# One decoder trunk, one change: a warmed opening, a written order around the last scan, weight tiles moved by 128 bytes, two output queues

## The chip, the core and the metric

The kernel runs on one core of one Trainium2 chip. The metric is the device time of one execution in microseconds (us). Three runs of the kernel before took 1699.51, 1695.92 and 1690.34 us, a median of 1695.92 us.

## What is computed

A trunk of four layers on 512 positions of width 1024, in float32: dilated attention, a gated FFN, a Mamba-2 scan mixer, a second gated FFN, then a last normalization. Cut to what matters:

```
for i in range(2):
    h = rmsnorm(x, mix_norm_w[i])
    if i == 0: x = x + dilated_attention_mixer(h, w_qkv, w_o, cos, sin)   # 3 groups of windows, 8 heads
    else:      x = x + ssd_mixer(h, w_in, ..., norm_w, w_out)             # 8 groups, 4 chunks of 128
    h = rmsnorm(x, ffn_norm_w[i])
    u = causal_depthwise_conv(h @ w_up, conv_w, conv_b)                   # 1024 -> 2 x 2816
    gate, up = u[..., :2816], u[..., 2816:]
    x = x + (silu(gate) * up) @ w_down
return rmsnorm(x, final_norm_w)
```

In the scan mixer a group's output `y` is gated, divided by the root mean square over its 256 channels, and multiplied by `w_out`.

## The kernel before

**Tiling.** Features stand on the 128 partitions and positions on the free axis, so x is eight tiles `xr[0..7]` of 128x512 and each weight unit is a 128x1024 tile, eight blocks of 128x128. Every large product is made of three matmuls (`mm3`, line 128): a float32 operand is split into a rounded part `h` and a remainder `l`, and the sum h·h + h·l + l·h is accumulated in one PSUM bank. Each of these matmuls has 512 columns and comes from one helper (line 126).

**Weights.** `load_unit` (line 107) loads a unit `raw` by DMA on SP's queue, casts it to `hi` on ACT (on DVE where it is loaded in pieces, which only the opening does) and subtracts to `lo` on DVE. There are four `hi` and four `lo` buffers and three `raw` ones.

**Rows.** `prep(k)` (line 169) turns one tile of x into the rows of the next product: `xh[k]` (ACT), `xl[k]` (DVE), its square (ACT) and the square's addition to `ssum` (POOL, line 182). When all eight are added, `inv_rms` sums over the partitions with matmuls against ones (`ss`, line 190), DVE scales (`ms`), POOL takes the power (`rcol`, line 195), and `along_free` (line 201) spreads the result with matmuls on an identity (`rb`). The product itself runs on rows that are not yet normalized; only its evacuation waits for `rb`.

**Stages.** The opening (lines 263 to 282) loads the eight tiles of x and the first four units of the values' weights, `v_steps`, in which the x tile is the stationary operand and the weights are the moving one (`v`, 96 matmuls a pass, four passes in all: two before the heads, two woven into them). Then come eight heads of attention (`qk`, `wo`), FFN 0 (`u`, `wd`), the scan mixer in eight groups (`xs`, `z`, `wso`, with the scan's own small matmuls `py`, `pf`, `pst`, `ss`, `prg`), and FFN 1. The output product of group 7, `wso70` to `wso77` (`write_groups([7])`), can't start before that group's `y70`, `y71` are normalized, and each `wso7m` must be added to `xr[m]` and prepared before the first product of FFN 1 can read `xh[m]`, `xl[m]`. `norm_and_project` (line 146) then does the first three units of FFN 1, `u1_0` to `u1_2`: seven eighths of the first two, the remaining eighths, `ss`, 15 matmuls of the third, `rb`.

**What sets the order.** A scheduler with a simulated timeline orders each engine's instructions; only inside `tc.manual_schedule` is an engine's order the one that is written. PSUM has three `mm` banks, three `aux` banks and two `side` banks.

**The end.** `finish` (line 805) does the last down products in two halves of 256 positions. For each half: `ss` over two operands in turn (lines 190 and 192), `rc`, `rb`, eight multiplications into four tiles `ot` (five on DVE at line 835, three on POOL at line 833), and four output DMAs, all on SP's queue (line 836).

## Time and profile before

| what | us | share |
|---|---|---|
| the three runs, median | 1695.92 | |
| the profiled execution, its own time | 1691.93 | |
| its span in the trace | 1690.1 | 100% |
| PE (matmuls), 8208 | 1658.2 | 98% |
| DVE, 1791 | 1085.5 | 64% |
| ACT, 1016 | 690.1 | 41% |
| POOL, 312 | 478.8 | 28% |
| DMA engines, mean | | 29% |

The page gives each engine's busy time, the granted TensorE clock in forty slices, the chain of work that ended last, and the costliest groups of instructions. The span is what the trace shows; the time of the execution is 1.8 us longer than it. PE is the engine to look at, so the views that matter are those of its timeline: where it is idle and for what, and how far apart the starts of two successive matmuls are, which is called the pitch here.

### The profile page before, as it was taken

Reading aid. Unit: us, or ns where it says so; the run is one execution under the profiler, and the core shown is the slowest. Engines: PE = TensorE matmul, PEld = TensorE weight load, DVE = VectorE, ACT = ScalarE, POOL = GpSimd, SP = SyncE. Lnnn points to the kernel's source line nnn. Section 1 sums busy time; section 2 is a strip of 40 time slices with the busy share of each in tenths; the row PEclk is TensorE's granted clock in tenths of the full one; section 3 lists DMA queues with packets and bytes.
Section 4 is the critical chain, followed back from the end, with each engine's and each line's share of the span. In section 5 each row is a group of like instructions: output and inputs, shape, how many; then the busy total and the mean of one; then the engine's idle time right before and its main releaser. Section 6 shows DMA issues by size and latency. Waiting matters only on the chain. (4 is left out here: it accounts for less than half of the span.)

```text
span 1690.1 us, 21485 instructions
## 1 busy us (share of the span) xinstructions
PE 1658.2 (98%) x8208; PEld 1399.0 (83%) x8208; DVE 1085.5 (64%) x1791; ACT 690.1 (41%) x1016; POOL 478.8 (28%) x312
## 2 busy tenths in 40 slices
PE   8999999999999999999999999999999999999997
PEld 6888888888888888888888788888887788888887
DVE  6365665366657745745657888788786774574565
ACT  4233332333344423433445665544562442342345
POOL 2344443044413211210231223232312421121124
PEclk9999999999999999999999999999999999999999
DMA  6222222222233223323233322233222222322324
GB/s 211 100 75 88 76 87 87 88 75 88 75 100 113 100 87 112 100 88 112 79 103 127 100 88 100 88 113 102 98 94 75 76 99 87 112 100 88 112 79 134
DMA packets 52343, 165.56 MB, mean 98 GB/s; under 512 B 5841, under 2 KB 8145, under 8 KB 52241
## 3 DMA queue, kind: packets, MB, share of 16 engines
q1 hardware_dynamic: 52240, 164.19, 29.0%
q8 instruction: 65, 1.06, 0.3%
q14 instruction: 38, 0.30, 0.1%
HBM read 162.01 MB, written 2.16 MB: 97 GB/s over the span
## 5 line engine op out<-in xcount | busy, mean ns | idle before, releaser
L126 PE MATMUL u<-xl,hi_u 128*128 128x512 f32 x704 | 271.3, 385 | 4.1 <-DVE xl L171 4.1
L126 PE MATMUL u<-xh,hi_u 128*128 128x512 f32 x704 | 271.1, 385 | 0.0
L126 PE MATMUL u<-xh,lo_u 128*128 128x512 f32 x704 | 270.8, 385 | 0.0
L517 POOL TENSOR_TENSOR au<-au,au 128x512 f32<-128x512 f32 x44 | 57.0, 1294 | 434.3 <-DVE au L497 413.7
L310 POOL TENSOR_TENSOR rotqk<-rotqk,sr 32x512 f32<-32x512 f32 x48 | 91.8, 1913 | 262.8 <-DVE rotqk L309 215.5
L117 ACT CAST hi_u<-raw_u 128x1024 fp32r<-128x1024 f32 x88 | 91.1, 1042 | 183.4 <-PE u L126 122.6
L497 DVE SCALAR_TENSOR_TENSOR au<-usu,par,au 128x511 f32<-128x511 f32 (+1 forms) x176 | 161.4, 921 | 6.4 <-ACT au L495 1.3
L126 PEld LDWEIGHTS u<-xl,hi_u 128*128 128x128 f32 x704 | 132.3, 188 | 30.8 <-DVE xl L171 5.6
L126 PEld LDWEIGHTS u<-xh,lo_u 128*128 128x128 f32 x704 | 132.4, 188 | 25.5
L126 PEld LDWEIGHTS u<-xh,hi_u 128*128 128x128 f32 x704 | 132.3, 188 | 25.4
L126 PE MATMUL qk<-xh,hi_qk 128*128 128x512 f32 x384 | 149.1, 388 | 0.0
L126 PE MATMUL qk<-xl,hi_qk 128*128 128x512 f32 x384 | 148.1, 386 | 0.0
L126 PE MATMUL qk<-xh,lo_qk 128*128 128x512 f32 x384 | 147.1, 383 | 0.0
L512 DVE TENSOR_TENSOR usu<-u,rbc 128x512 f32<-128x512 f32 x88 | 60.7, 691 | 118.0 <-PE u L126 111.5
L118 DVE TENSOR_TENSOR lo_u<-raw_u,hi_u 128x1024 fp32r<-128x1024 f32 x88 | 110.0, 1254 | 26.9 <-ACT hi_u L117 26.9
L530 DVE TENSOR_TENSOR xr<-xr,wd 128x512 f32<-128x512 f32 x40 | 27.2, 687 | 117.1 <-PE wd L126 117.1
L117 ACT CAST hi_qk<-raw_qk 128x1024 fp32r<-128x1024 f32 x48 | 50.2, 1046 | 127.9 <-PE qk L126 73.1
L117 ACT CAST hi_wd<-raw_wd 128x1024 fp32r<-128x1024 f32 (+1 forms) x56 | 52.5, 953 | 119.1 <-PE wd L126 74.8
L306 DVE TENSOR_TENSOR qk<-qk,cr 128x512 f32<-128x512 f32 x48 | 33.0, 688 | 91.0 <-PE qk L126 90.8
L182 POOL TENSOR_TENSOR ssum<-ssum,sq 128x512 f32<-128x512 f32 (+1 forms) x40 | 56.0, 1400 | 106.8 <-ACT sq L181 105.8
L126 PEld LDWEIGHTS qk<-xh,lo_qk 128*128 128x128 f32 x384 | 72.0, 188 | 13.2
L126 PEld LDWEIGHTS qk<-xh,hi_qk 128*128 128x128 f32 x384 | 72.1, 188 | 12.8
(631 smaller groups left out, 4013.0 us busy)
## 6 DMA issues: line engine op xcount, KB each, us to landing
raw_u<-in_wup SPq DMA_DIRECT2D x88, 512.0 KB, 3.2
raw_qk<-in_wqk SPq DMA_DIRECT2D x48, 512.0 KB, 3.2
raw_wd<-in_wdn SPq DMA_DIRECT2D x32, 512.0 KB, 3.2
raw_wd<-in_wdn SPq DMA_DIRECT2D x24, 384.0 KB, 3.0
raw_xs<-in_win SPq DMA_DIRECT2D x16, 512.0 KB, 3.3
raw_z<-in_win SPq DMA_DIRECT2D x16, 512.0 KB, 3.2
lm<-rows SPq DMA_DIRECT2D x32, 256.0 KB, 3.7
raw_wso<-in_wso SPq DMA_DIRECT2D x16, 512.0 KB, 3.2
```

The source lines that it names most:

```text
L117: SC.copy(hi[:, s], raw[:, s])
L118: low.tensor_tensor(lo[:, s], raw[:, s], hi.bitcast(F32)[:, s], op=ALU.subtract)
L126: T.matmul(in_turns(dst), w, in_turns(x), start=first, stop=last)
L182: G.tensor_tensor(ssum, ssum, sq, op=ALU.add)
L306: V.tensor_tensor(at(t), of(p), of(cr), op=ALU.mult)
L310: G.tensor_tensor(rot[R, :], rot[R, :], sr[R, :], op=ALU.mult)
L497: V.scalar_tensor_tensor(dst[:, j:], src[:, : S - j], col(c_w + taps - 1 - j), dst[:, j:], op0=ALU.mult, op1=ALU.add,)
L512: V.tensor_tensor(us, p, rbc, op=ALU.mult)
L517: G.tensor_tensor(ab[1], ab[0], ab[1], op=ALU.mult)
L530: V.tensor_tensor(xr[m], xr[m], p, op=ALU.add)
```

## The change

- **Opening.** Eight matmuls of `ones` on `ones` (`warm`) stand first on PE. `prep` is divided into `split` (`xh`, `xl`) and `square`; the opening writes all the splits first, and the seven additions of squares go to DVE instead of POOL. The second half of each unit's `hi` is cast on ACT instead of DVE (four casts).
- **Weight tiles.** `hi` and `lo` are 1088 elements wide in place of 1024, and the values' units start 32 elements (128 bytes) into them. A smaller DMA scratch makes the room. Every tile's address changes with it.
- **`inv_rms`.** All matmuls over the first operand, then all over the second; one start and one stop for the bank.
- **Last scan.** `last_group` writes PE's order by hand from the second half of group 7's scan on: the group's sum of squares (`ss`) stands behind `wso55`, its `prg` between `wso56` and `wso57`; `u1_0` to `u1_2` are woven into `wso73` to `wso77`, with `u1_1` and `u1_2` in the two `side` banks; the FFN's `ss` comes behind all 72 matmuls of these three. The two casts `y70h`, `y71h` are written ahead of the two subtractions `y70l`, `y71l`.
- **Output.** Of each half's four output DMAs, two are issued on ACT's queue.

Everything else keeps its order, apart from two swaps of neighbours on DVE and one on SP.

```diff
-    def load_unit(src, name, n=1024, pieces=1, low=V):
+    def load_unit(src, name, n=1024, pieces=1, low=V, at=0):
...
-        hi = wh.tile([P, 1024], F32R, tag="hi", name=f"hi_{name}")
-        lo = wh.tile([P, 1024], F32R, tag="lo", name=f"lo_{name}")
+        hi, lo = (wh.tile([P, 1088], F32R, tag=t, name=f"{t}_{name}")[:, at : at + 1024] for t in ("hi", "lo"))
...
-            if pieces > 1:
+            if i < pieces - 1:
                 V.tensor_copy(hi[:, s], raw[:, s])
             else:
                 SC.copy(hi[:, s], raw[:, s])
...
-    def square(k, src, ssum):
+    def square(k, src, ssum, add=G):
...
-            G.tensor_tensor(ssum, ssum, sq, op=ALU.add)
+            add.tensor_tensor(ssum, ssum, sq, op=ALU.add)
...
-        for j in range(cn):
-            js = slice(j * P, (j + 1) * P)
-            T.matmul(p[:, j : j + 1], ssum[:, js], ones[:, 0:1], start=True, stop=more is None)
-            if more is not None:
-                T.matmul(p[:, j : j + 1], more[:, js], ones[:, 0:1], start=False, stop=True)
+        parts = [ssum] if more is None else [ssum, more]
+        for i, part in enumerate(parts):
+            for j in range(cn):
+
+                T.matmul(
+                    p[:, j : j + 1], part[:, j * P : (j + 1) * P], ones[:, 0:1], start=i == 0 and j == 0,
+                    stop=i == len(parts) - 1 and j == cn - 1, skip_group_check=True,
+                )
...
-                state[u] = load_unit(A["wv"][((g - 1) * 2 + half) * 4 + u], f"{n}{u}", pieces=pieces)
+                state[u] = load_unit(A["wv"][((g - 1) * 2 + half) * 4 + u], f"{n}{u}", pieces=pieces, at=32)
...
+    warm = side_bank("warm")
+    for _ in range(8):
+        T.matmul(warm[:, 0:P], ones, ones, start=True, stop=True)
...
-            prep(k, xp, C_MIX, ssum)
+            split(k, xp, C_MIX)
+            xps.append(xp)
...
+    for k, xp in enumerate(xps):
+        square(k, xp, ssum, V)
...
+    def last_group():
...
+        scan = scan_group(NSG - 1, tiles[NSG - 1], ys)
+        weave(scan, 3, ahead[NSG - 1][4:] + w4 + w56[:4])
+        load7, w7 = write_groups([7], ys)
+        with tc.manual_schedule(engines={mybir.EngineType.PE}):
+            next(scan)
+            w56[4]()
+            w56[5]()
+            next(scan)
+            w56[6]()
+            load7(0)
...
+            with tc.manual_schedule(engines={mybir.EngineType.DVE, mybir.EngineType.Activation}):
+                next(scan, None)
+                w56[7]()
+                unit(0)
+                load7(1)
+            w7[0]()
+            w7[1]()
+            w7[2]()
+            part(0, 0)
+            w7[3]()
+            part(0, 1)
+            part(1, 0, 1)
+            w7[4]()
+            part(0, 2)
+            part(1, 2)
+            part(2, 0)
+            w7[5]()
...
+            w7[7]()
+            part(2, 4)
+            for k in range(5, KD):
+                for i in range(3):
+                    part(i, k)
+            inv_rms(ssum_b, D, rcol)
+            part(3, *range(4))
+            p = along_free(rcol, "rb")
+            SC.copy(rbc, p)
+            part(3, *range(4, KD))
...
-                dma(out[k : k + 2, :, ts].rearrange("k p t -> p k t"), ot.rearrange("p (k t) -> p k t", k=2))
+                queue = nc.sync if k % 4 == 0 else nc.scalar
+                queue.dma_start(out[k : k + 2, :, ts].rearrange("k p t -> p k t"), ot.rearrange("p (k t) -> p k t", k=2))
...
-    nc = bacc.Bacc("TRN2", target_bir_lowering=False, num_devices=1)
+    nc = bacc.Bacc("TRN2", target_bir_lowering=False, num_devices=1, dynamic_dma_scratch_size=1024)
```

Three places show how the built programs differ. A row is an instruction: its line, its operation, what it writes and what it reads. The first place is DVE in the opening, from its first work on; `hi_v`, `lo_v` are the values' weights, `xl` the remainders of x. Before:

```order
L115 CAST hi_v_114<-raw_v_113 128x512
L171 SCALAR_TENSOR_TENSOR xl_90<-xp_108,par,xh_82 128x512
L118 TENSOR_TENSOR lo_v_115<-raw_v_113,hi_v_114 128x512
L115 CAST hi_v_114<-raw_v_113 128x512
L118 TENSOR_TENSOR lo_v_115<-raw_v_113,hi_v_114 128x512
L171 SCALAR_TENSOR_TENSOR xl_91<-xp_122,par,xh_83 128x512
L115 CAST hi_v_165<-raw_v_164 128x512
L171 SCALAR_TENSOR_TENSOR xl_92<-xp_157,par,xh_84 128x512
L115 CAST hi_v_165<-raw_v_164 128x512
L118 TENSOR_TENSOR lo_v_166<-raw_v_164,hi_v_165 128x512 x2
L171 SCALAR_TENSOR_TENSOR xl_93<-xp_173,par,xh_85 128x512
```

And after:

```order
L116 CAST hi_v_122<-raw_v_121 128x512
L176 SCALAR_TENSOR_TENSOR xl_90<-xp_117,par,xh_82 128x512
L119 TENSOR_TENSOR lo_v_123<-raw_v_121,hi_v_122 128x512 x2
L176 SCALAR_TENSOR_TENSOR xl_91<-xp_130,par,xh_83 128x512
L186 TENSOR_TENSOR ssum<-ssum,sq 128x512
L116 CAST hi_v_167<-raw_v_166 128x512
L176 SCALAR_TENSOR_TENSOR xl_92<-xp_162,par,xh_84 128x512
L186 TENSOR_TENSOR ssum<-ssum,sq 128x512
L119 TENSOR_TENSOR lo_v_168<-raw_v_166,hi_v_167 128x512 x2
L176 SCALAR_TENSOR_TENSOR xl_93<-xp_175,par,xh_85 128x512
L186 TENSOR_TENSOR ssum<-ssum,sq 128x512
```

One cast of every unit has left DVE's row, and one addition of squares has come in behind each `xl` from the second on.

The second place is DVE at the end of the last scan, where `yt` are the two halves of group 7's output, `wso57` is the last product of groups 5 and 6, and `lo_u1_*`, `lo_wso71` are remainders of weights. Before:

```order
1253 L754 SCALAR_TENSOR_TENSOR yt_10106<-yt_10106,par_76,prg_10307 128x512
1254 L754 SCALAR_TENSOR_TENSOR yt_10188<-yt_10188,par_76,prg_10307 128x512
1255 L118 TENSOR_TENSOR lo_u1_0_10480<-raw_u1_0_10478,hi_u1_0_10479 128x1024
1256 L775 TENSOR_TENSOR xr7_3979<-xr7_3979,wso57_10350 128x512
1257 L757 TENSOR_TENSOR y70l_10314<-yt_10106,y70h_10313 128x512
1258 L118 TENSOR_TENSOR lo_u1_1_10487<-raw_u1_1_10485,hi_u1_1_10486 128x1024
1259 L757 TENSOR_TENSOR y71l_10319<-yt_10188,y71h_10318 128x512
1260 L775 TENSOR_TENSOR xr0_3972<-xr0_3972,wso70_10370 128x512
1261 L775 TENSOR_TENSOR xr1_3973<-xr1_3973,wso71_10381 128x512
```

And after:

```order
1255 L769 SCALAR_TENSOR_TENSOR yt_10153<-yt_10153,par_76,prg_10354 128x512
1256 L769 SCALAR_TENSOR_TENSOR yt_10275<-yt_10275,par_76,prg_10354 128x512
1257 L773 TENSOR_TENSOR y70l_10361<-yt_10153,y70h_10360 128x512
1258 L773 TENSOR_TENSOR y71l_10365<-yt_10275,y71h_10364 128x512
1259 L793 TENSOR_TENSOR xr7_3988<-xr7_3988,wso57_10369 128x512
1260 L119 TENSOR_TENSOR lo_u1_0_10385<-raw_u1_0_10383,hi_u1_0_10384 128x1024
1261 L793 TENSOR_TENSOR xr0_3981<-xr0_3981,wso70_10397 128x512
1262 L119 TENSOR_TENSOR lo_wso71_10392<-raw_wso71_10390,hi_wso71_10391 128x1024
1263 L119 TENSOR_TENSOR lo_u1_1_10455<-raw_u1_1_10453,hi_u1_1_10454 128x1024
1264 L793 TENSOR_TENSOR xr1_3982<-xr1_3982,wso71_10408 128x512
1265 L176 SCALAR_TENSOR_TENSOR xl0_90<-xr0_3981,par_76,xh0_82 128x512
```

The two subtractions now follow the two `yt` at once, and what stood between them, with `lo_wso71` besides, now stands ahead of `xr1` and `xl0`.

The third place is PE where the first product of FFN 1 begins. Before, behind the last row of `wso77`:

```order
5515 L126 MATMUL wso77_10465<-y71l_10319,hi_wso71_10421 128x4x32x4
5516 L126 MATMUL wso77_10465<-y71h_10318,lo_wso71_10422 128x4x32x4
5517 L126 MATMUL u1_0_10484<-xh0_82,hi_u1_0_10479 128x4x32x4
5518 L126 MATMUL u1_0_10484<-xl0_90,hi_u1_0_10479 128x4x32x4
5519 L126 MATMUL u1_0_10484<-xh0_82,lo_u1_0_10480 128x4x32x4
5520 L126 MATMUL u1_0_10484<-xh1_83,hi_u1_0_10479 128x4x32x4
```

And after, behind the last row of `wso72`:

```order
5486 L127 MATMUL wso72_10421<-y71l_10365,hi_wso70_10347 128x4x32x4
5487 L127 MATMUL wso72_10421<-y71h_10364,lo_wso70_10348 128x4x32x4
5488 L127 MATMUL u1_0_10389<-xh0_82,hi_u1_0_10384 128x4x32x4
5489 L127 MATMUL u1_0_10389<-xl0_90,hi_u1_0_10384 128x4x32x4
5490 L127 MATMUL u1_0_10389<-xh0_82,lo_u1_0_10385 128x4x32x4
5491 L127 MATMUL wso73_10437<-y70h_10360,hi_wso70_10347 128x4x32x4
```

The first rows that need `xh0`, `xl0` stand 30 matmuls earlier, three at a time between the remaining `wso7` products.

## Rows read from the trace of the kernel before

**Rows 1.** The page: PE's busy time, share of the span, instructions.

```profile
PE 1658.2 (98%) x8208; PEld 1399.0 (83%) x8208; DVE 1085.5 (64%) x1791; ACT 690.1 (41%) x1016; POOL 478.8 (28%) x312
```

**Rows 2.** Waits of PE, whole span: us in total, times, longest us.

```profile
PE v L126 <- ACT ssum L178: 5.3, 1, 5.3
PE u L126 <- DVE xl L171: 4.1, 3, 2.4
```

**Rows 3.** Stretches: length, PE busy (instructions), PEld, DVE, ACT, POOL, granted clock, DMA, GB/s.

```profile
5.31:11.31 6.00, 6.00 (x14) 4.74 (x15) 5.43 (x7) 3.32 (x6) 2.67 (x2) 1.00 0.96 339
...
1253.76:1257.17 3.41, 3.41 (x10) 2.73 (x10) 3.06 (x5) 3.38 (x5) 0.28 (x1) 0.50 0.02 5
1299.40:1330.66 31.26, 25.86 (x101) 19.19 (x99) 22.42 (x24) 14.13 (x22) 11.49 (x7) 0.89 0.21 68
1318.61:1325.44 6.83, 4.47 (x10) 3.08 (x11) 4.35 (x3) 0.04 (x1) 3.06 (x2) 0.50 0.22 77
```

**Rows 4.** Chain that ended last, near FFN 1's start: start, us, engine, output.

```profile
1330.66 0.79 PE ss L190 x8
...
1407.50 42.88 PE wd L126 x192
```

**Rows 5.** PE in the opening: start, us, operation, count, idle before and releaser.

```profile
5.31 2.04 PE L126 MATMUL v<-hi_v,xh 128*128 128x512 f32 x4 [5.31 <-ACT ssum L178]
...
20.44 0.49 PE L126 MATMUL v<-hi_v,xl 128*128 128x512 f32 x1 [0.60 <-DVE xl L171]
...
33.37 1.05 PE L201 MATMUL rb<-ident,rcol 128*128 128x128 f32 x8
34.18 0.47 PE L126 MATMUL v<-hi_v,xh 128*128 128x512 f32 x1
```

**Rows 6.** DVE and POOL in the opening, same columns.

```profile
10.06 1.76 DVE L171 SCALAR_TENSOR_TENSOR xl<-xp,par,xh 128x512 fp32r<-128x512 f32 x1
...
12.08 3.48 DVE L118 TENSOR_TENSOR lo_v<-raw_v,hi_v 128x512 fp32r<-128x512 f32 x2
...
22.84 0.74 DVE L171 SCALAR_TENSOR_TENSOR xl<-xp,par,xh 128x512 fp32r<-128x512 f32 x1
...
11.76 8.07 POOL L182 TENSOR_TENSOR ssum<-ssum,sq 128x512 f32<-128x512 f32 x5 [0.49 <-ACT sq L181]
```

**Rows 7.** PE where value products give way to `qk`, and back.

```profile
56.48 0.38 PE L126 MATMUL qk<-xh,hi_qk 128*128 128x512 f32 x1
...
88.17 0.38 PE L126 MATMUL v<-xh,hi_v 128*128 128x512 f32 x1
```

**Rows 8.** PE at the last scan's end.

```profile
1299.43 0.38 PE L126 MATMUL wso<-y61h,lo_wso 128*128 128x512 f32 x1
...
1301.71 0.49 PE L126 MATMUL wso<-y70h,hi_wso 128*128 128x512 f32 x1 [1.03 <-DVE xr L775]
...
1318.46 0.68 PE L126 MATMUL u<-xl,hi_u 128*128 128x512 f32 x1 [1.22 <-DVE xl L171]
...
1322.35 0.80 PE L126 MATMUL u<-xl,hi_u 128*128 128x512 f32 x1 [2.36 <-DVE xl L171]
```

**Rows 9.** DVE and POOL beside it.

```profile
1301.57 0.68 DVE L757 TENSOR_TENSOR y70l<-yt,y70h 128x512 fp32r<-128x512 f32 x1
1302.17 1.22 DVE L118 TENSOR_TENSOR lo_u<-raw_u,hi_u 128x1024 fp32r<-128x1024 f32 x1
...
1320.55 2.41 DVE L171 SCALAR_TENSOR_TENSOR xl<-xr,par,xh 128x512 fp32r<-128x512 f32 x2
...
1318.27 3.48 POOL L182 TENSOR_TENSOR ssum<-ssum,sq 128x512 f32<-128x512 f32 x2 [0.42 <-ACT sq L181]
```

**Rows 10.** The end: PE's last sums, SP's output DMAs.

```profile
1681.06 0.36 PE L190 MATMUL ss<-ones,ssum 128*128 128x1 f32 x2
1681.28 0.36 PE L192 MATMUL ss<-ones,sq 128*128 128x1 f32 x2
...
1684.63 1.98 SPq L836 DMA_DIRECT2D out<-ot  x4
```

More of the change, by code (lines that the diff above doesn't have):

```diff
@@ L169, in prep, with split @@
     def prep(k, src, c_w, ssum):
+        split(k, src, c_w)
+        square(k, src, ssum)
+    def split(k, src, c_w):
         SC.activation(xh[k], src, AF.Copy, scale=col(c_w + k))
@@ L764, in write_groups, with load @@
         units = {}
+        def load(i):
+            if i not in units:
+                units[i] = [load_unit(A["wso"][2 * g + i], f"wso{g}{i}") for g in gs]
         def step(m):
             i, at = divmod(m, 4)
-            if i not in units:
-                units[i] = [load_unit(A["wso"][2 * g + i], f"wso{g}{i}") for g in gs]
+            load(i)
             p = mm_bank(f"wso{gs[0]}{m}")
@@ L777, in step @@
                 prep(m, xr[m], C_FFN + KD, ssum_b)
-        return [lambda m=m: step(m) for m in range(KD)]
+        return load, [lambda m=m: step(m) for m in range(KD)]
     ys = []
@@ L784, in trunk @@
     weave(decay_rates(), 3, ahead[0])
-    w01, w23, w4, w56 = (write_groups(gs, ys) for gs in ([0, 1], [2, 3], [4], [5, 6]))
+    w01, w23, w4, w56 = (write_groups(gs, ys)[1] for gs in ([0, 1], [2, 3], [4], [5, 6]))
     writes = [[], [], w01[:4], w01[4:], w23[:4], w23[4:], [], w4 + w56]
-    for g in range(NSG):
-        a, w = ahead[g + 1] if g < NSG - 1 else ahead[g][4:], writes[g]
+    for g in range(NSG - 1):
+        a, w = ahead[g + 1], writes[g]
         if g == NSG - 2:
             a = a[:4]
-        if g == NSG - 1:
-            fill = a + w
-        else:
-            n = -(-len(w) // len(a))
-            fill = []
-            for i, f in enumerate(a):
-                fill += [f] + w[i * n : (i + 1) * n]
-        weave(scan_group(g, tiles[g], ys), 6, fill)
@@ L800, in trunk, with unit, part @@
-    for f in write_groups([7], ys):
-        f()
-    norm_and_project(ssum_b, up_first(1))
+        n = -(-len(w) // len(a))
+        fill = []
+        for i, f in enumerate(a):
+            fill += [f] + w[i * n : (i + 1) * n]
+        weave(scan_group(g, tiles[g], ys), 6, fill)
+    def last_group():
[9 more added lines that the diff above has]
+            load7(0)
+            units = []
+            def unit(i):
+                name = f"u1_{i}"
+                units.append((
+                    load_unit(A["wup"][44 + i], name), side_bank(name) if i in (1, 2) else mm_bank(name), name
+                ))
+            def part(i, *ks):
+                if i == len(units):
+                    unit(i)
+                (hi, lo), t, _ = units[i]
+                for k in ks:
+                    mm3(t, hi, lo, k, xh[k], xl[k], k == 0, k == KD - 1)
+            with tc.manual_schedule(engines={mybir.EngineType.DVE, mybir.EngineType.Activation}):
[15 more added lines that the diff above has]
+            w7[5]()
+            part(0, 3)
+            part(1, 3)
+            part(2, 1, 2)
+            w7[6]()
+            part(0, 4)
+            part(1, 4)
+            part(2, 3)
+            w7[7]()
[8 more added lines that the diff above has]
+            part(3, *range(4, KD))
+        for _, t, name in units:
+            early[name] = t
@@ L805, in finish @@
+    last_group()
     def finish(load, operand, cn):
```

8 lines of the change are left out of this document (4 added, 4 removed).

## The prediction

> **What bounds the kernel now.** PE is busy for 1658.2 of 1690.1 us [rows 1]. So I read the waits of PE first: no wait of the whole kernel is longer than 5.3 us, and only a few of them lie where the change works: the first matmul (5.3 us) and `u` waiting for `xl` (4.1 us in three waits) [rows 2]. The busy share hides a second loss, though: PE also counts as busy while its matmuls run slowly. The stretches show it. From 5.31 to 11.31 us only 14 matmuls ran, 0.43 us each, while the down products of FFN 1 run 192 in 42.88 us, 0.2233 us each [rows 3, 4]. I use 0.2233 us as the full pitch. Two later stretches, 3.41 us at 1253.76 and 6.83 us at 1318.61, have a granted clock of 0.50, and there a matmul takes the same 0.43 us [rows 3]. The column of the granted clock says 1.00 for the opening; I go by the pitch there, which is that of the half clock (1.2 of 2.4 GHz).
>
> For each place I therefore take the time from one matmul's start to a later one's, subtract matmuls times 0.2233 us, and call the remainder the excess. Only excess can be won: the number of large matmuls does not change.
>
> **Opening.** The stretch from 5.31 us to the first matmul behind `rb` at 34.18 us takes 28.87 us [rows 5]. It holds 96 value matmuls (21.44 us), and `ss` and `rb` with some 0.8 us each (`rb` from 33.37 to 34.18 [rows 5]); that makes 23.05. The excess is 5.8 us. Of this, 14 × (0.4286 − 0.2233) = 2.9 us is the half clock [rows 3]. Some 0.3 is the values' pitch, treated below. The remaining 2.6 or so are waits for data like the one at 20.44, where PE waits for `xl` [rows 5], and the slow restarts behind them.
>
> The waits come from DVE. While POOL adds squares, five additions in 8.07 us, an `xl` takes 1.76 us and two `lo_v` take 3.48; once POOL is done an `xl` takes 0.74 [rows 6], and a subtraction of this size takes 0.68 [rows 9]. The two contended rows alone lose 1.0 + 2.1 us; over the whole opening I count about 7 us in that way (an estimate from the same differences). The change takes POOL out. It gives DVE seven additions, 7 × 0.65 = 4.5 us, and takes four casts off it, some 1.5 us (estimates; the addition by the subtraction's 0.68, the cast at somewhat above half of that). So DVE is ahead of the old order by about 7 − 4.5 + 1.5 = 4 us near the end of the opening, which is more than the 2.6 us of waits: I cost them at nothing afterwards. The four casts land on ACT. One of them, and the casts of the next units, stand ahead of the evacuation of the first four value banks; 20 and more matmuls of the next pass cover that, and if the cover fails it costs a cast, about 1 us.
>
> The eight `warm` matmuls have no like in the trace at that place. `rb` is eight such passes and takes 1.05 us [rows 5], so 16 passes take 2.1 us at full clock and some 4 at half; they can start when `ones` is set, near 1 us, and so are over by 5.3 us, while data arrive. They add nothing to the path. What they bring is the clock: in this run it rose 6.0 us after PE's first matmul (5.31 to 11.31). If it again takes 6.0 us from the first work of PE, it rises near 7.1 instead of 11.3, and 4 matmuls instead of 14 run slowly: 2.0 us won. Bounds: nothing (it rises at 11.3 as before) and 2.9 us (full from the first real matmul). I take 2.0, since the work stands ahead almost without a gap. Opening together: 2.6 − 0.3 for remaining small waits + 2.0 = 4.3 us, bounds 2.3 and 5.5.
>
> **Values' weights shifted by 128 bytes.** The second pass of `v` runs 96 matmuls from 34.18 to 56.48 [rows 5, 7]: 0.2323 us each. The `qk` products behind it run 144 from 56.48 to 88.17: 0.2201 us each [rows 7]. Same clock, same shape, so something other than columns sets the pitch, and the values' products, where weights are the moving side, are the ones that take longer. In the built program the moving operand's address less the stationary one's, modulo 256 bytes, is 192 for these products before and 64 after; for `qk` it is 64 both times. If that is the cause, the second pass wins 96 × 0.009 to 0.012 = 0.9 to 1.2 us; the two later passes, at about 0.227, win 192 × 0.004 to 0.007 = 0.7 to 1.3; the first some 0.3. I take 1.9 us, bounds 0 and 3.2; a loss of up to 1 us (one step of 3 ns on 384 matmuls) can't be excluded, as nothing here explains the steps.
>
> The Trainium skill ("TensorE: Matmul & The Clock Gate", Step-by-step: what each phase is for) gives PE two independent read ports, one for the moving rows and one for the weights, and puts 512 columns at about 216 ns back to back whatever the addresses. By that rule the shift wins nothing and the forecast would be 1.9 us higher. The 232 and 220 ns of one stage speak against it, without saying what else it is.
>
> **Last scan.** Before, PE starts the last `wso57` matmul at 1299.43 and `ss` at 1330.66 [rows 4, 8]: 31.23 us for 97 matmuls (48 of `wso7`, 48 of `u1`), which would be 21.66. The excess is 9.6 us: waits for `xr` and `y70l` at the start of `wso70` (1.03 us in the row, and `y70l` itself waits on DVE until 1301.57), waits for `xl` of 0.5, 1.22 and 2.36 us, and the half clock behind them [rows 3, 8, 9]. DVE is late there because POOL adds squares beside it: two `xl` take 2.41 us where one takes 0.74 [rows 6, 9].
>
> After, `y70l`, `y71l` follow `yt` at once; walking DVE's new row with these durations they are ready within about 0.3 us of the end of `wso57`, so the first wait goes. The rows for `xl` then have far more cover: 72 `u1` matmuls stand between and behind the `wso7` products, and each eighth of x is needed only after the other two units' parts of the eighth before. One wait is new: `u1_0` asks for `xl0` behind 18 `wso7` matmuls, at 1299.7 + 4.0 = 1303.7, while DVE, free from about 1299.9, has `xr7`, `lo_u1_0`, `xr0`, `lo_wso71`, `lo_u1_1` and `xr1` ahead of `xl0`: three additions of 0.6, three subtractions of 1.15 and `xl0` at 0.74 (0.6 from one start to the next and 1.22 in [rows 9], 0.74 in [rows 6]) make 6.0, so `xl0` is there near 1305.8. What is queued behind the waiting matmul on PE is `wso73`, whose data are there. This costs about 1.9 us. So PE reaches the end of 72 `u1` at 1299.43 + 121 × 0.2233 + 1.9 = 1328.4. The old order would have done the same work by 1330.66 + 24 × 0.2233 = 1336.0. Won: 7.6 us. Bounds: if the new wait halves the clock for one stretch like that at 1253.76 (3.41 us, losing half of it, 1.7) and POOL's additions slow DVE as before so that two more waits of 1.2 us appear, 7.6 − 4.1 = 3.5; without the new wait 9.5. Behind `ss` 30 matmuls, 6.7 us, cover `rcol` before `rb`, where 15 did before, so nothing is lost there. The wait of `ss` for the group's squares at 1252.9 and its half clock stay as they are.
>
> **End.** `ss` over the first operand no longer stands between the two of the second: one pair, 0.22 us [rows 10], leaves the path. The output DMAs are issued in 1.98 us by one queue [rows 10]; I estimate that the data's way out is nearly as long, so the second queue wins 0 to 0.15. Together 0.3 us.
>
> **Sum.** 4.3 + 1.9 + 7.6 + 0.3 = 14.1 us. The profiled execution took 1691.93 us, so it would take 1677.8. The median of the three runs, 1695.92, is 4.0 us above the profiled one; carried over, 1681.9. I forecast 1682 us. The terms' bounds, each taken from the value chosen and added as squares, give 2.7 us below and 5.0 above; with some 3 us for the spread of the runs shown its own range is 1677 to 1688.
>
> **Rivals.** (a) *The pitch of all products moves up.* Every tile's address changes, and the pitch takes steps near 3.3 ns (0.2201, 0.2233, 0.2323 [rows 4, 7]) for reasons the profile doesn't show. There are some 6,500 matmuls of 512 columns; one step up on all of them costs 6,500 × 3.3 ns = 21.5 us and takes the 1.9 us of the shift with it, and the kernel would take 1682 + 21.5 + 1.9 = 1705.4 us, slower than before. It decides from 14.1 / 6,500 = 2.2 ns a matmul; the place to see it is FFN 0 and FFN 1, where nothing else changes. For it: two stages of the same work differ. Against: the addresses of the other products, moving against stationary, keep their difference. Chance 0.07. (b) *The same step down* on about half of the products, with `qk`'s 0.2201 as what is possible: 1682 − 10.5 = 1671.5. Chance 0.08. (c) *The new wait for `xl0` stands for the old ones*: the last scan wins only its lower bound, 3.5 us, by the halved clock and DVE slowed beside POOL; 1686. For it: POOL's additions stay where they are in this part. Against: three units share each `xl`. Chance 0.15. (d) *The warm matmuls and the shift do nothing*: 1682 + 2.0 + 1.9 = 1686. For it: the clock's rise has one example at this place only, and the address is a guess. Chance 0.10.
>
> **Chances.** That leaves 0.60 for the forecast. I call over 0.5% (below 1687.4 or above 1704.4) a change, about what a measurement of this kernel can tell from none. Faster: nearly all of 0.60 and of (b), and most of (c) and (d): 0.81. Same: the rest of these, and (a) where it touches only a part of the products: 0.14. Slower: the rest of (a), 0.05. The range, 1673 to 1690, leaves out (a), most of (b) and little at either end of the rest.
>
> **What would show it.** Opening right: no wait of PE for `xl` or `lo_v` before 34 us, POOL without additions, `xl` at 0.74 us throughout, full pitch from near 7 us, first matmul behind `rb` at 29.5 to 30. Shift right: the second value pass at 0.223 us or less. Last scan right: no idle time before `wso70`, one wait of about 2 us for `xl0`, no `xl` wait behind it, `ss` some 7.5 us earlier against the work done. Wrong: a half clock behind the new wait, several waits for `xl` between `wso73` and `wso77`, or a changed pitch in the FFNs, which would outweigh all the rest.

## The result

The changed kernel took 1679.75 us in the median of four runs (1678.58 to 1681.40), the kernel before 1694.87 us in four (1690.34 to 1699.51). The ratio is 0.9911, with a 95% interval of 0.9882 to 0.9941: 0.9% faster. The forecast was 1682 us with a range of 1673 to 1690. The profiled execution of the changed kernel took 1678.81 us; the sum had come to 1677.8 for it.

The two traces, put side by side at the same places of the program, show where the time went:

| the start of | before, us | after, us | after less before | won in between |
|---|---|---|---|---|
| first value matmul | 5.31 | 5.34 | +0.03 | |
| first matmul behind `rb` | 34.18 | 29.08 | -5.10 | 5.13 (opening) |
| first `qk` | 56.48 | 50.60 | -5.88 | 0.78 (second value pass) |
| FFN 0's `rb` | 532.39 | 525.87 | -6.52 | 0.64 (heads, with the third and fourth pass) |
| last `wso57` matmul | 1299.43 | 1293.66 | -5.77 | -0.75 (scan mixer) |
| first `wd` of FFN 1 | 1407.34 | 1393.88 | -13.46 | 7.69 (last scan and start of FFN 1) |
| last `rb` | 1682.68 | 1669.06 | -13.62 | 0.16 |
| end of the span | 1690.14 | 1677.03 | -13.11 | -0.51 |

Inside the stretch of the heads, the third and the fourth value pass became 0.60 us shorter from the first of their matmuls to the last (43.88 us before, 43.28 after).

### The profile page after: what moved, and what is told of

Its sections match the earlier page's. It is cut to its first block, busy times and chain, and to the rows that moved or that the text cites. A ratio compares the mean times of both kernels' runs of the same rounds, so it can differ in the third digit from the quotient of the medians.

```text
span 1677.0 us, 21515 instructions
## 1 busy us (share of the span) xinstructions
PE 1654.9 (99%) x8224; PEld 1401.9 (84%) x8224; DVE 1075.1 (64%) x1794; ACT 693.2 (41%) x1020; POOL 469.9 (28%) x305
## 3 DMA queue, kind: packets, MB, share of 16 engines
q10 hardware_dynamic: 1088, 1.05, 0.2%
## 5 line engine op out<-in xcount | busy, mean ns | idle before, releaser
L512 DVE SCALAR_TENSOR_TENSOR au<-usu,par,au 128x510 f32<-128x510 f32 (+1 forms) x176 | 162.2, 926 | 6.6 <-ACT au L510 1.7
L127 PEld LDWEIGHTS qk<-xl,hi_qk 128*128 128x128 f32 x384 | 72.1, 188 | 12.3
```

Of the source, the lines that this page charges most:

```text
L127: T.matmul(in_turns(dst), w, in_turns(x), start=first, stop=last)
L512: V.scalar_tensor_tensor(dst[:, j:], src[:, : S - j], col(c_w + taps - 1 - j), dst[:, j:], op0=ALU.mult, op1=ALU.add,)
```

## The profile after

The page, as in [rows 1]: PE is still the engine that sets the time.

```profile
span 1677.0 us, 21515 instructions
...
PE 1654.9 (99%) x8224; PEld 1401.9 (84%) x8224; DVE 1075.1 (64%) x1794; ACT 693.2 (41%) x1020; POOL 469.9 (28%) x305
```

The waits of PE over the whole span, as in [rows 2] (us in total, times, longest). `u` waits once for `xl` where it waited three times for 4.1 us, and the first value matmul waits 0.5 us behind the warm matmuls, where it waited 5.3 us from the start of the span:

```profile
PE u L127 <- DVE xl L176: 1.8, 1, 1.8
...
PE v L127 <- ACT ssum L182: 0.5, 1, 0.5
```

PE in the opening, as in [rows 5] (start, us, operation, count, idle before). The eight warm matmuls, of float32, show as 16 passes. No row between 5.34 and 28.17 us has an idle time, the groups of four start 0.88 us apart from 6.88 us on, and the work behind `rb` starts at 29.08:

```profile
1.05 3.78 PE L275 MATMUL warm<-ones 128*128 128x128 f32 x16 [1.05 <-DVE mhalf L100]
5.34 1.70 PE L127 MATMUL v<-hi_v,xh 128*128 128x512 f32 x4 [0.51 <-ACT ssum L182]
6.88 1.04 PE L127 MATMUL v<-hi_v,xl 128*128 128x512 f32 x4
7.76 1.04 PE L127 MATMUL v<-lo_v,xh 128*128 128x512 f32 x4
...
28.17 1.16 PE L208 MATMUL rb<-ident,rcol 128*128 128x128 f32 x8
29.08 0.47 PE L127 MATMUL v<-hi_v,xh 128*128 128x512 f32 x1
...
50.60 0.38 PE L127 MATMUL qk<-xh,hi_qk 128*128 128x512 f32 x1
...
82.28 0.38 PE L127 MATMUL v<-xh,hi_v 128*128 128x512 f32 x1
```

DVE in the opening, as in [rows 6]: an `xl` takes 0.74 us and two subtractions 1.28, with POOL idle, against 1.76 and 3.48 before.

```profile
9.62 0.74 DVE L176 SCALAR_TENSOR_TENSOR xl<-xp,par,xh 128x512 fp32r<-128x512 f32 x1
...
10.89 1.28 DVE L119 TENSOR_TENSOR lo_v<-raw_v,hi_v 128x512 fp32r<-128x512 f32 x2
```

Stretches, as in [rows 3] (length, PE busy and its instructions, PEld, DVE, ACT, POOL, granted clock, DMA, GB/s). The half clock behind 1249 us is the one of before; one at 934.98 is new, the one at the last scan is gone, and the one at the end begins ahead of the last `rb` (1668.85 us, `rb` at 1669.06), where in the kernel before it began behind it (1683.84 us, `rb` at 1682.68):

```profile
934.98:938.39 3.41, 3.41 (x23) 2.80 (x22) 3.20 (x6) 1.38 (x3) 0.00 (x0) 0.50 0.17 36
1249.01:1252.42 3.41, 3.41 (x10) 2.66 (x9) 2.73 (x6) 3.40 (x5) 1.01 (x1) 0.50 0.17 43
1293.66:1322.44 28.78, 26.96 (x123) 22.63 (x121) 20.14 (x24) 15.95 (x23) 10.31 (x7) 1.00 0.27 92
1668.85:1677.00 8.15, 1.23 (x4) 0.93 (x4) 1.74 (x5) 0.37 (x1) 2.25 (x4) 0.50 0.39 129
```

PE at the last scan, as in [rows 8], and DVE beside it, as in [rows 9]. `wso70` follows the last `wso57` at once; the one wait is for `xl0`, which DVE starts only after `lo_wso71`, `lo_u1_1` and `xr1`:

```profile
1293.66 0.39 PE L127 MATMUL wso<-y61h,lo_wso 128*128 128x512 f32 x1
1293.88 0.38 PE L127 MATMUL wso<-y70h,hi_wso 128*128 128x512 f32 x1
...
1300.10 0.48 PE L127 MATMUL u<-xl,hi_u 128*128 128x512 f32 x1 [1.82 <-DVE xl L176]
...
1322.44 0.95 PE L196 MATMUL ss<-ones,ssum 128*128 128x1 f32 x8
```

```profile
1296.43 1.22 DVE L119 TENSOR_TENSOR lo_wso<-raw_wso,hi_wso 128x1024 fp32r<-128x1024 f32 x1
1297.57 1.22 DVE L119 TENSOR_TENSOR lo_u<-raw_u,hi_u 128x1024 fp32r<-128x1024 f32 x1
1298.71 0.68 DVE L793 TENSOR_TENSOR xr<-xr,wso 128x512 f32<-128x512 f32 x1
1299.30 0.74 DVE L176 SCALAR_TENSOR_TENSOR xl<-xr,par,xh 128x512 fp32r<-128x512 f32 x1
...
1300.56 2.44 DVE L176 SCALAR_TENSOR_TENSOR xl<-xr,par,xh 128x512 fp32r<-128x512 f32 x2
```

The last `rb` runs at half clock, 1.23 us:

```profile
1669.06 1.23 PE L208 MATMUL rb<-ident,rc 128*128 128x128 f32 x4 [1.04 <-POOL rc L202]
```

## Experiments

The theory: the opening wins by the clock and by taking POOL from beside DVE; the shift wins by the address; the last scan wins by its order, less one new wait that DVE's order makes. The main rival throughout: what looks like an edit's gain is a difference between two executions. The runs `no_warm`, `adds_pool`, `no_warm_adds_pool`, `shifts`, `ffn_shifts` and `ffn_break` are one execution each, so they are read by their places and not by their time, since the changed kernel's own times lie up to 4.8 us apart. Two edits of the change were not tried alone: the four casts on ACT and the order inside `inv_rms`.

### The warm matmuls, and the second queue

```diff
-    for _ in range(8):
-        T.matmul(warm[:, 0:P], ones, ones, start=True, stop=True)
...
-                queue = nc.sync if k % 4 == 0 else nc.scalar
+                queue = nc.sync
```

> The changed kernel without the eight warm matmuls, and with all output DMAs on one queue again. Theory (the clock): the warm matmuls alone bring the early clock. Without them the clock rises some 6 us after the first value matmul, near 11 us; about 14 value matmuls run at 0.43 us instead of 3, and since DVE stays free of POOL no wait for data appears. The first matmul behind rb moves from 29.08 us to 31.4 (31.0 to 31.8). Rival (the data): the early clock came with denser data, not with the warm matmuls; then the clock rises before 9 us and the matmul behind rb starts before 30 us. Output: one queue costs 0 to 0.15 us between the first ot and the end of the span (6.25 us with two); the rival says 0.5 or more.

The half-clock pitch lasts to 8.36 us, seven matmuls (a stretch of this kernel, and its PE behind `rb`):

```profile
5.33:8.36 3.03, 3.03 (x7) 2.46 (x8) 1.78 (x3) 1.27 (x3) 0.00 (x0) 1.00 0.79 287
```

```profile
30.04 0.47 PE L127 MATMUL v<-hi_v,xh 128*128 128x512 f32 x1
```

The work behind `rb` starts at 30.04 us, 0.96 later than with the warm matmuls, not 2.3. That lies just beyond the rival's bound; what it disproves is the fixed 6.0 us of the forecast. It doesn't show that the warm matmuls are worth 0.96 us: nine profiles with this opening unaltered have this start anywhere from 28.82 to 30.29 us. What speaks for the mechanism is the count of value matmuls at half clock: 7, 8 and 14 in the three profiles without warm matmuls, none to 4 in ten of the eleven with them, and 8 in the eleventh (`shifts`).

From the last `rb` to the end of the span it took 7.48 us here with one output queue, 7.46 in the profile of before and 7.45 to 7.48 in the eleven others with two queues and a full clock at `rb`: the second queue is worth nothing that shows. In both kernels the 1.05 MB of the last half's output moved for about 3.1 us at 310 to 370 GB/s, longer than one queue's 1.98 us of issuing.

### The additions back on POOL

```diff
-        square(k, xp, ssum, V)
+        square(k, xp, ssum, G)
```

> The changed kernel with the seven additions of squares in the opening back on POOL; the warm matmuls and the casts on ACT stay. Theory (POOL beside DVE): while POOL adds, xl takes about 1.7 us again instead of 0.74 and a subtraction about 1.7 instead of 0.68; DVE is about 2.5 us later at its last xl than with its own seven additions, PE waits for xl and lo_v again for 1.5 to 2.5 us in all, and the first matmul behind rb starts at 30.5 to 31.6 us instead of 29.08. Rival (slack): the four casts that left DVE are enough cover; no wait over 0.3 us appears and the matmul behind rb starts before 29.6.

PE's waits between 5 and 34 us, a row of POOL and two of DVE, and PE behind `rb`:

```profile
PE v L127 <- DVE xl L176: 2.1, 2, 1.3
PE v L127 <- DVE lo_v L119: 0.5, 1, 0.5
```

```profile
8.97 10.93 POOL L186 TENSOR_TENSOR ssum<-ssum,sq 128x512 f32<-128x512 f32 x7 [8.52 <-ACT sq L185]
```

```profile
10.50 1.78 DVE L176 SCALAR_TENSOR_TENSOR xl<-xp,par,xh 128x512 fp32r<-128x512 f32 x1
...
22.57 0.74 DVE L176 SCALAR_TENSOR_TENSOR xl<-xp,par,xh 128x512 fp32r<-128x512 f32 x1
```

```profile
32.89 0.47 PE L127 MATMUL v<-hi_v,xh 128*128 128x512 f32 x1
```

The waits are back (2.6 us), as the theory said, and the cost is larger than it said: 3.8 us, from 29.08 to 32.89, and 2.6 against the latest of the nine starts with the additions on DVE. As long as POOL adds, an `xl` takes 1.78 us; once POOL is done it takes 0.74.

### Both undone

```diff
-        T.matmul(warm[:, 0:P], ones, ones, start=True, stop=True)
...
-        square(k, xp, ssum, V)
+        square(k, xp, ssum, G)
```

> The changed kernel without the warm matmuls and with the additions of squares on POOL; of the opening's edits only the casts on ACT and the shift stay. Theory (the two edits add up): with warm matmuls POOL's additions cost 3.8 us (29.08 to 32.89), without additions on POOL the missing warm matmuls cost 1.0 (29.08 to 30.04), so the first matmul behind rb starts at 33.9 us (33.4 to 34.4; 34.18 in the kernel before). Rival (the waits for data hide what the clock gives): 32.9 to 33.2, since a PE that runs faster only waits longer for xl.

The work behind `rb` starts at 35.07 us, 2.2 us after the kernel with warm matmuls and POOL, more than the sum of the two: behind a wait of 1.2 us for `lo_v` the clock fell once more (the stretch from 22.22, in which a matmul took twice the time, so that about half of its 3.41 us was lost).

```profile
22.22:25.63 3.41, 3.41 (x10) 2.65 (x9) 3.41 (x5) 1.05 (x1) 0.00 (x0) 0.50 0.55 201
```

So POOL's additions cost 3.8 us with the warm matmuls and 5.0 without, the second with that half clock in it. For the missing warm matmuls the two pairs give 1.0 and 2.2 us, from one execution each: the first lies inside the spread of 1.5 us, and most of the second is that stretch.

### Other offsets for the values' weights

```diff
-pieces=pieces, at=32)
+pieces=pieces, at={(1, 0): 0, (2, 0): 0, (1, 1): 16, (2, 1): 64}[g, half])
```

> The changed kernel with other offsets of the values' weights inside their tiles: 0 bytes in the first and the second value pass, 64 bytes in the third, 256 bytes in the fourth (128 everywhere in the changed kernel); the order of instructions is the same. Theory (the address difference modulo 256 bytes sets the pitch): first pass 0.226 us (0.220 with 128 bytes), second 0.232 (0.2233), fourth as with no shift, 0.227 (0.2233); the third in between. The first matmul behind rb moves by 0.6 us and qk's first by 1.4. Rival (not the address): the pitches stay 0.220, 0.223, 0.224, 0.223 within 0.001, and the gain came from the other changes around them.

The second pass, 96 matmuls between these two rows of PE, took 22.30 us, as long as before the change, 0.2323 us each:

```profile
31.52 0.47 PE L127 MATMUL v<-hi_v,xh 128*128 128x512 f32 x1
...
53.82 0.38 PE L127 MATMUL qk<-xh,hi_qk 128*128 128x512 f32 x1
```

Mean pitch of the four passes, without the few starts over 0.3 us apart: 0 bytes 0.2312 and 0.2317, 64 bytes 0.2263, 256 bytes 0.2315; with 128 bytes in the changed kernel 0.2202, 0.2233, 0.2243, 0.2233. In all twelve profiles with 128 bytes the second pass lay between 0.2200 and 0.2240, the third at 0.2243 and the fourth at 0.2233, so in these three the offset sets the pitch, and in the fourth 256 bytes are worse than 128. The first pass tells nothing: with 128 bytes it ran at up to 0.2361 in other executions (below). The theory's 0.227 for the fourth pass was wrong. Modulo 256 bytes an offset of 256 is that of the kernel before, which had 0.2267 there, and not 0.2315: that difference alone doesn't fix the pitch.

### Offsets for the FFNs' weights

```diff
+    offsets = {"u0": (0, 4, 60), "u1": (8, 56, 48), "wd0": (0, 4, 60), "wd1": (8, 56, 0)}
```

(in elements of four bytes, by part of the FFN.)

> The changed kernel with offsets for the FFN weights inside their tiles, the order of instructions unchanged. Up weights of FFN 0 by 0, 16 and 240 bytes in its three parts, of FFN 1 by 32, 224 and 192 (but for its first three units); down weights of FFN 0 by 0, 16, 240, of FFN 1 by 32, 224, 0. Theory (the address difference modulo 256 bytes sets the pitch of every product, as it does for the values): the parts with 0 stay at 0.2233 us, some of the others move by one step of 3.3 ns or more, up or down; those at 192 and 224 are the likeliest to slow down. Rival (only products whose weights move are sensitive): all parts stay at 0.2233 within 0.0005.

Stretches of `u` with offsets of 0, 32, 224 and 192 bytes, in that order. The counts take in one or two matmuls that began before the stretch, so the pitch is taken from the first start inside to the last:

```profile
540.00:598.00 58.00, 58.00 (x261) 48.67 (x260) 41.82 (x44) 25.25 (x33) 18.49 (x13) 1.00 0.29 98
1345.00:1395.00 50.00, 50.00 (x224) 41.48 (x223) 41.06 (x43) 24.40 (x33) 17.85 (x13) 1.00 0.31 106
1450.00:1525.00 75.00, 75.00 (x325) 60.62 (x324) 49.60 (x53) 30.85 (x40) 19.72 (x13) 1.00 0.30 99
1590.00:1640.00 50.00, 50.00 (x210) 39.11 (x209) 31.23 (x35) 20.70 (x27) 14.60 (x10) 1.00 0.23 80
```

That is 0.2233, 0.2254, 0.2317 and 0.2400 us (the 384 `u` matmuls at 224 bytes run from 1441.40 to 1530.36 us, the 288 at 192 bytes from 1574.84 to 1643.94); the down products at 32 and 224 bytes had 0.2254 and 0.2316, and the parts with 16 and 240 bytes stayed at 0.2233. Full clock everywhere, the same instructions: only an address differs, and 192 bytes cost 17 ns a matmul. In every other profile but `ffn_break` these parts ran at 0.2233; each new offset was run once. The kernel took 1692.51 us.

### The last scan ordered as before

```diff
-    last_group()
+        weave(scan_group(g, tiles[g], ys), 6, fill)
+    for f in write_groups([7], ys)[1]:
+        f()
+    norm_and_project(ssum_b, up_first(1))
```

> The changed kernel with the last scan, wso70 to wso77 and the start of FFN 1 ordered as before the change; everything else stays. Theory (the waits at the last scan): the whole gain of that place goes back. From the last wso57 matmul to the first matmul of FFN 1's first wd takes 107.3 to 108.0 us as before, instead of 100.2; waits of PE for xr, y70l and xl of 4 to 6 us in all and a stretch at half clock stand there again. The time is about 7 us over the changed kernel's. Rival (the place gains little by itself and the clock's luck made the difference): less than 4 us between the two.

PE's waits between 1285 and 1337 us are those of before:

```profile
PE u L127 <- DVE xl L176: 4.6, 3, 3.0
PE wso L127 <- DVE xr L793: 1.0, 1, 1.0
```

From the last `wso57` to the first `wd` it took 107.94 us (107.91 before, 100.23 after), with a half clock behind the third wait. The median was 1688.04 us, ratio to the kernel before 0.997 (0.9927 to 1.0013). In this stretch the order is worth 7.7 us against the first profile of the changed kernel, 5.7 against its two later ones (below); the rest of the change alone can't be told from none by the time.

### `xl0` earlier on DVE

```diff
+            with tc.manual_schedule(engines={mybir.EngineType.DVE}):
+                w7[0](later=True)
+                w7[1](later=True)
+                prep(0, xr[0], C_FFN + KD, ssum_b)
                 load7(1)
...
+                prep(1, xr[1], C_FFN + KD, ssum_b)
+                unit(1)
```

> The changed kernel with another order on DVE at the start of wso70: xr0, xr1, xl0 come first, and the remainders lo_wso71 and lo_u1_1 behind them; PE's order is the same. Theory (the new wait is made by DVE's order): the wait of 1.82 us for xl0 falls to 0.4 or less, no wait of u for xl over 0.5 us takes its place, and from the last wso57 matmul to the first wd of FFN 1 it takes 98.5 to 99.0 us instead of 100.2. Rival (POOL's additions slow DVE, so xl is late anyway): the wait moves to xl1 or xl2 and more than 1 us of waiting stays.

PE's waits of `u` in the same stretch, and the `xl1` that it waits for:

```profile
PE u L127 <- DVE xl L176: 0.5, 1, 0.5
```

```profile
1298.13 1.77 DVE L176 SCALAR_TENSOR_TENSOR xl<-xr,par,xh 128x512 fp32r<-128x512 f32 x1
```

The wait of 1.82 us for `xl0` is gone, and one of 0.51 us for `xl1` has come, whose subtraction stood beside POOL's first addition. That is the rival's mechanism at a smaller size than its 1 us. The stretch from the last `wso57` to `ss` fell only from 28.78 to 28.26 us, and the one to the first `wd` from 100.23 to 99.79, less than expected: in the changed kernel's first profile the `u` matmuls behind the wait had run at 0.2200 us, here they ran at 0.2238. The time was 1677.65 us, ratio 0.9908 (0.9885 to 0.993), which can't be told from the changed kernel's 0.9911.

### `xl1` earlier too

```diff
-                load7(1)
                 prep(1, xr[1], C_FFN + KD, ssum_b)
+                load7(1)
```

> As xl0_first, with xl1 also ahead of lo_wso71 on DVE. In xl0_first the wait for xl0 was gone, but one of 0.51 us for xl1 had come, since xl1 took 1.77 us beside POOL. Theory (DVE's order makes the waits): no wait of u for xl over 0.3 us is left, at most one of up to 0.6 us for lo_u1_1, and from the last wso57 matmul to ss it takes 27.6 to 28.2 us at a pitch of 0.2233 (28.26 in xl0_first, 28.78 in the changed kernel, there with 72 products at 0.220). Against the changed kernel on the same chip 0.5 to 2 us less. Rival (the sum of DVE's and POOL's work is the limit): the wait only moves, the stretch stays within 0.2 us of 28.26.

```profile
PE u L127 <- DVE lo_u L119: 1.3, 1, 1.3
```

```profile
1297.35 2.31 DVE L119 TENSOR_TENSOR lo_wso<-raw_wso,hi_wso 128x1024 fp32r<-128x1024 f32 x1
```

The rival's mechanism came: the wait moved to `lo_u1_1`, 1.31 us, since `lo_wso71` ahead of it on DVE now stood beside POOL's first addition and took 2.31 us for 1.22. The stretch to `ss` was 29.15 us, longer than either side expected; behind the wait the matmuls ran at 0.2283 us, which is some 0.4 us of it. The time was 1678.54 us, ratio 0.9909 (0.9891 to 0.9926).

### The additions at the last scan on DVE

```diff
-                prep(m, xr[m], C_FFN + KD, ssum_b)
+                split(m, xr[m], C_FFN + KD)
+                square(m, xr[m], ssum_b, V)
```

(with `xl0` and `xl1` early, as in `xl0_first`.)

> The changed kernel with xl0 and xl1 early on DVE as in xl0_first, and with the seven additions of squares of this place on DVE instead of POOL, so that POOL has nothing beside DVE between wso70 and ss. Theory (POOL beside DVE is what makes xl or lo_u1_1 late): each xl takes 0.74 us and each 1024-wide remainder 1.22, no wait of u over 0.3 us is left, and from the last wso57 matmul to ss it takes 27.2 to 27.6 us (121 matmuls at 0.2233 are 27.02; 28.26 in xl0_first). Rival (DVE has no room for seven more additions): a wait of u for xl2, lo_u1_2 or a later xl of over 0.7 us appears, or ss waits for the last addition, and the stretch stays above 28 us.

```profile
PE u L127 <- DVE xl L176: 0.3, 1, 0.3
```

Every `xl` took 0.74 or 0.75 us, one wait of 0.27 us was left, and the stretch took 27.81 us, the shortest of all, a little over the 27.6 expected. The theory holds: POOL beside DVE makes the data late, and DVE has room for the seven additions. The time was 1678.78 us against 1680.07 of the changed kernel on the same chip (ratios to the kernel before 0.9911, 0.9897 to 0.9924, and 0.9924, 0.9911 to 0.9936): 1.3 us less, but the intervals overlap.

### The changed kernel again

> The changed kernel once more, for the comparison on one chip and as a second look at what varies with the same program. The clock theory (dips come by chance of phase) expects the same waits of PE within 0.1 us, but the half clock behind other ones of them than in the first profile, and the clock's rise in the opening anywhere from 4 to 9 us. The rival (dips belong to places) expects the half clock behind the same two waits again, near 935 and 1249 us, and the rise at 6.5.

> The changed kernel on the same chip as the run before it, to compare their times, and a third look at the draws of the same program. Expected of the theory that half clock and pitch are drawn anew in every execution: the waits of PE repeat within 0.1 us, the stretches of half clock stand behind others of them than at 935 and 1249 us or at 1248 and 1302.6, and the first value pass has a pitch other than one of the two seen (0.2200 and 0.236), or either of them. Expected of the rival that a program has one pattern: the first or the second profile repeats in all of these.

Medians of 1679.86 and 1680.07 us. Three executions of one program, with the same waits of PE to within 0.25 us but for two at `prg` and `pst`, and yet spans of 1677.0, 1680.5 and 1680.8 us. The half clock stood behind the waits at 935 and 1249 us in the first, at 1248 (6.83 us long) and 1302.6 in the second, at 486.9, 937.5, 1251.5 and 1302.7 in the third. Two stretches of the second, and the first value pass of the third:

```profile
1302.60:1306.00 3.40, 3.40 (x9) 2.65 (x8) 2.79 (x4) 2.26 (x4) 3.22 (x2) 0.50 0.39 157
5.51:25.00 19.49, 19.49 (x83) 15.83 (x84) 17.73 (x29) 13.89 (x21) 0.00 (x0) 1.00 0.90 322
```

```profile
5.62:25.00 19.38, 19.38 (x86) 15.89 (x86) 17.50 (x29) 13.89 (x21) 0.00 (x0) 1.00 0.94 322
```

The first value pass ran at a mean of 0.2202, 0.2361 and 0.2280 us, though no address differed and, but for 0.3 to 0.5 us ahead of its first matmul, no wait stood in it. The rival, that a program has one pattern, falls. What differs so from one execution to the next, with nothing changed, is called drawn below.

### A break in the FFN's stream

```diff
             p = along_free(rcol, "rb")
             SC.copy(rbc, p)
+            T.matmul(aux_bank("brk")[:, 0:1], ones, rbc[:, 0:1], start=True, stop=True)
```

> The changed kernel with five extra one-column matmuls: three behind rb (FFN 0, the scan mixer, FFN 1), the first two of them waiting 0.6 us or more for ACT's copy of rb, and two in the second part of each FFN, which wait for nothing. In every profile so far the FFNs ran at 0.2233 us behind rb, while other stretches ran at 0.2200 in some profiles and at 0.2233 in others, with the same program. Theory (a wait of PE draws the pitch anew, and it stays until the next break): behind the waiting matmul in FFN 0 the pitch may be 0.2200 for hundreds of matmuls, which gives up to 4 us in FFN 0. Rival (the FFN's products can only run at 0.2233): no stretch of FFN 0 behind the break is below 0.222, and the extra matmuls cost about 0.1 us each and the two waits 0.6 to 0.9.

The added matmul behind `rb` waited 0.68 us for ACT's copy. FFN 0 in two stretches, before and behind the second, not waiting extra matmul near 650 us:

```profile
540.00:598.00 58.00, 58.00 (x256) 47.59 (x255) 40.23 (x43) 25.16 (x33) 16.96 (x12) 1.00 0.30 100
660.00:725.00 65.00, 65.00 (x292) 54.51 (x291) 45.10 (x49) 27.54 (x36) 18.07 (x13) 1.00 0.30 99
```

Behind the waiting matmul the pitch was 0.2283 us, from start to start, for 120 us, then 0.2233 from the next break on; in FFN 1 it was 0.2233 behind the first of the two and 0.2227 behind the second. In this one execution the pitch changed at the breaks and was kept between them, as the theory said, but this draw was a bad one: no stretch of FFN 0 behind the break went below 0.2233, and the rival's price of the edit was exceeded. It was 1685.56 us.

## Why the prediction held, point by point

**Direction and size.** 14.1 us were summed, 13.1 found between the two traces. That the sum is so near is in part luck: the opening gave more than forecast, the shift and the end less, and the scan mixer, which stood at nothing, lost 0.75. The two later profiles of the same program are 3.5 and 3.8 us longer than the one set against the sum.

**Opening: 4.3 us forecast, and 0.3 more for the pitch; 5.1 measured.** For the data the mechanism was right and the size too small: the waits were put at 2.6 us with their restarts, from an execution in which PE itself ran at half clock to 11.31 us, and putting the additions back on POOL cost 3.8 and 5.0 us. With the clock up at 6.76 us PE waited 2.6 us for `xl` and `lo_v`, against 1.3 in the kernel before, as one expects of a PE that asks sooner. The data edit carries most of the gain: without the warm matmuls the opening still won 4.1 of the 5.1 us. The clock was put at 2.0 by one example (6.0 us from PE's first work). In ten further profiles with warm matmuls, and the changed kernel's own, the full pitch began between 4.2 and 9.1 us; in the three without, at 8.36, 8.57 and 11.31. So an earlier clock is likely but not certain in one execution, and no run shows that it is worth 2.0: the moment of the rise is drawn, and part of the gain may go in waits. In three of the profiles in which it rose before 5.5 us, PE then waited 0.3 to 0.8 us for an `xh` of ACT. The predicted range for the work behind `rb`, 29.5 to 30.0, was missed by the first profile (29.08); all with this opening unaltered lie at 28.8 to 30.3.

**Shift: 1.9 us forecast, 1.4 measured in passes two to four, the first open.** The other offsets show that the address is the cause in the second and the fourth pass: 0 and 256 bytes bring 0.232 there. The upper bound of 3.2 is more than the 2.8 to which the term's own parts add up. The Trainium skill ("TensorE: Matmul & The Clock Gate", Step-by-step: what each phase is for) would have given 0 in every case; the trace disagrees, with 0.2233 and 0.2400 us for the same FFN product at offsets of 0 and 192 bytes. In the first pass the pitch was 0.220, 0.236 and 0.228 in three executions of the same program, so what the shift gives there isn't settled.

**Last scan: 7.6 us forecast, 7.7 measured.** Each step was found: no wait before `wso70`, one new wait (2.0 forecast, 1.82 measured), no other wait for `xl`, `ss` at 28.78 us behind the last `wso57` where 28.97 was worked out. Ordering the place as before gave all of it back. One reading was a little off: `ss` began at 1330.50 us in the trace of before, and the chain's 1330.66 is where the matmul ahead of it ended, so the old order's excess was 9.4 us rather than 9.6. Rival (c) was half right: its mechanism, a half clock behind the new wait, is absent from the first profile, but present in the two later ones of the same program, where the stretch to the first `wd` took 102.2 and 102.3 us in place of 100.2. So the term is 7.7 us without that half clock and 5.7 with it, and some 0.4 of the 7.7 is luck: behind the wait the first profile drew a pitch of 0.2200 us, and `no_warm`, with the same order, no half clock there and 0.2240, took 29.17 us to `ss` and 100.64 to the first `wd`.

**Scan mixer: nothing forecast, 0.75 us lost.** The half clock at 934.98 us, behind a wait of 2.1 us that the kernel before has as well. It isn't of the change: of the fourteen profiles nine have it there and five do not, the one of before and one of the changed kernel among these.

**End: 0.3 us won was forecast, 0.35 lost.** The order of `ss` gave 0.16 (from the first `wd` to the last `rb` 275.18 us, 275.34 before), the second queue nothing: from the first `ot` to the end it took 6.26 us with two, 6.26 before and 6.28 in `no_warm` with one. The forecast had the data's way out nearly as long as the issues, 1.98 us; it took about 3.1. The rest is 0.51 us for an `rb` at half clock, 1.23 us where 0.71 stands in the profile without warm matmuls. In the thirteen other profiles, that of before among them, `rb` and what follows took 7.45 to 7.48 us, in this one 7.97. The sign of the term was an accident of one execution.

**The rivals on the pitch of all products.** Neither came: FFN 0 took 72.58 us from the start of `rb` to the first `wd` in both kernels, 0.2233 us a matmul. The offsets for the FFNs show that rival (a) was no fancy: other addresses cost up to 17 ns a matmul. What the prediction named against it fits: in the built programs the addresses of the other products, moving against stationary, keep their difference of 64 bytes modulo 256. Rival (d) fell for the shift; for the warm matmuls it stays open.

## What to carry to other kernels

An order is best judged by its places, not by the time of the kernel: here PE's waits repeated to 0.25 us from one execution to the next but for two, where the time moved by 4. A stretch moves too, by 2 us at the last scan and 1.5 in the opening, with the clock and the pitch, so an edit worth less than that wants more than one profile. Take work off an engine that slows the one PE waits for, and look at both edits of a pair together, since a faster consumer meets a late supplier. And before an address is changed for room, look at the pitch of the products that read it.

## What the hardware showed

- **Where the weights lie in SBUF against the rows changes the pitch of a 512-column matmul at full clock:** 0.2233 us at the FFN's own offset, 0.2254 at 32 bytes more, 0.2317 at 224, 0.2400 at 192. In the values' second pass 0.2317 at 0 (two profiles) and 0.2200 to 0.2240 at 128 (twelve); in the fourth 0.2267 at 0, 0.2315 at 256 and 0.2233 at 128; in the third 0.2275 at 0, 0.2264 at 64 and 0.2243 at 128. When all weight tiles moved and the difference of the addresses stayed, the pitch stayed (`qk` 0.220, FFNs 0.2233).
- **At one address there are several pitches:** in `wo`'s stretch near 500 us 0.2200 in seven profiles, 0.2233 in six and 0.2227 in one; 0.220, 0.228 and 0.236 in the first value pass; 0.2283 for 120 us of FFN 0 behind an added one-column matmul, 0.2233 behind the next, which suggests that a pitch lasts until a break in the stream. Behind `rb` FFN 0 ran at 0.2233 in every profile but that one. What decides the draw stays open.
- **Whether a wait of PE is followed by half clock differs between executions of one program.** The wait of 2.1 us ahead of `wo` was followed by it in five profiles of fourteen, that of 1.82 us for `xl0` in five of the nine that have it, that of 1.6 to 1.7 us for `prg` near 1010 us in none of the thirteen that have it. In three executions of the changed kernel itself, the 2.1 us ahead of `wo` were followed by it once, the 1.82 us twice.
- **Beside POOL's additions DVE's operations on two SBUF tiles take about twice as long:** `xl` 0.74 us alone and 1.76 to 1.78 beside them, a 1024-wide subtraction 1.22 and 2.31. POOL's addition takes some 1.28 us at its shortest, and two of them 3.42 beside two `xl`; DVE's addition of `wso`, which reads one operand from PSUM, stayed at 0.68 beside them. This agrees with the Trainium skill ("SBUF — State Buffer", SBUF: two separate sides), where these two share a port; the same section has PE never waiting for anyone, which the pitches above leave doubtful, though no run here shows a port as their cause.
